# A fourth softmax tile, and slope tables made by halving the one before, in a differential-attention decoder layer

## Chip, core and metric

The kernel runs on one core of a Trainium2 chip. The metric is the device time of one execution in microseconds (us), as the median of several runs. Beside it stands one profiled execution, whose trace gives every instruction's start and duration.

## What is computed

One decoder layer over 1024 tokens of width 1024: three branches (differential attention, pooling, cross-attention to 256 memory tokens), merged by gates and an output product, then a channel mixer. All is float32. The change touches the differential attention alone (8 heads, two softmax maps per head, width 64 each):

```python
def one_block(args):                    # 128 queries at a time
    qblk, i = args
    qpos = i * Q_BLOCK + jnp.arange(Q_BLOCK)
    s = jnp.einsum('bqhcd,bkhcd->bhcqk', qblk, kf) * scale
    dist = qpos[:, None] - kpos[None, :]
    bias = -slopes[:, None, None] * dist.astype(jnp.float32)   # slopes: 2 ** -(h + 1)
    s = s + bias[None, :, None]
    s = jnp.where((dist >= 0)[None, None, None], s, jnp.finfo(jnp.float32).min)
    p = jax.nn.softmax(s, axis=-1)
    a = p[:, :, 0] - lam * p[:, :, 1]
    return jnp.einsum('bhqk,bkhe->bqhe', a, vf)
```

Each head's output is then normalized per token, and all heads enter one product (the attention branch's merge).

## The kernel before

Each matmul of the layer's large products is done as three products of rounded halves (`mm3`, lines 103 to 105, high x high, low x high, high x low). A framework places the tiles and schedules: the code names the instructions, and a list scheduler with estimated durations sets the order in which they stand on each engine's queue; each engine then runs its queue strictly in that order and waits where an operand or a buffer is not ready. `tc.issue_after` adds edges by hand.

Attention runs head by head (h = 0 to 7). A head has eight query blocks of 128 tokens, t = 2b + u, in four pairs b; block t sees n = (t + 1) x 128 keys, so the last blocks of a head have n = 896 and n = 1024. For a block:

- `products` (L1185, tile `pss`): TensorE makes both maps' scores, c = 0 and 1, each in a pair of PSUM banks. There are two such pairs (`ps2`, bufs 2).
- `scores` (L1210): VectorE adds the head's slope table `hbias` to the scores, writes the sum into the SBUF tile `z` (tag `z0` for the first map, `z1` for the second), and keeps the row minimum in `mx`. In `order` rows this instruction is ISA, in the profile CUSTOM_DVE_ANT_0. Then ScalarE takes the exponential in place (L1219) and sums the row.
- `combine` (L1236 to L1239): VectorE subtracts the second map, weighted, from the first, into the first map's tile. That tile (`z0`) therefore lives on until the block's weights are transposed; the second map's (`z1`) is free after the combine.
- `turn_weights` (L1255, tile `pta`): TensorE transposes the pair's weights in groups of up to four into PSUM banks (`ps1`, two banks, shared with `poa` and `pn`); ScalarE copies a group rounded (L99, `aT`), VectorE subtracts for the low half (L100), which frees the bank.
- `weigh_values` (L1274, `poa`): TensorE weighs the values; ScalarE copies the output and its square (L1276, L1280, L1282).
- `head_norm` (L1299, `pn`): sums of squares by a product with ones; ScalarE copies the row (L1301) and GpSimd's queue stores it.

Pair b's transposes and weighing stand a stage behind its scores, and the next head's first blocks follow without a break. Between them the scheduler spreads filler products: the next head's keys (`head_keys`, L103 to L105 into `pqk`, 24 matmuls for each half of the tokens; `hTh_110` is the first half, `hTh_111` the second), and gates (`gate`, into `pg`) in head 0, in head 7 and after it. After attention the heads' outputs are loaded, scaled (L1527) and split into `ath` and `atl`, and the merge (`pya`) begins.

The slope tables: GpSimd makes `bias` once (L1060, L1062), a table of minus-distances with a huge value where a key lies ahead of the query. For each head ScalarE makes a scaled copy, `hbias` (L1067, two buffers), one head ahead: head h + 1's in stage b = 1 of head h. All these tiles are in the pool `att`: `bias` and `hbias` 4608 bytes per partition each, a `z` 4096 bytes; there were three `z0` and two `z1`.

Of the kernel before, what the change touches and what calls it, by code (L numbers as in the profile page):

```python
# [8 lines left out]
F32 = mybir.dt.float32  # L9
F32R = mybir.dt.float32r  # L10
I32 = mybir.dt.int32
AF = mybir.ActivationFunctionType
# [3 lines left out]
P = 128  # L16
D = 1024
S = 1024
# [23 lines left out]
def kernel(  # L42
# [7 lines left out]
    nc = tc.nc  # L50
# [12 lines left out]
    out = out[0]  # L63
# [293 lines left out]
    with tc.tile_pool(name="kvm", reuse_waits="tile", bufs=1, side="right") as kvp:  # L357
# [5 lines left out]
        with tc.tile_pool(name="pa", reuse_waits="tile", bufs=2, side="right") as pa, \  # L363
# [22 lines left out]
            with tc.issue_after(begun.ins):  # L386
                table = nc.scalar.activation(out=small.tile([P, 1], F32, tag="sm", name="table"), in_=epsilon,
                                             func=AF.Sqrt)
# [82 lines left out]
            for i in range(2):  # L471
                on("dve", lambda: nc.vector.tensor_scalar(
                    out=rcol[:, i, :], in0=ident, scalar1=0.0, scalar2=rm[i], op0=ALU.mult, op1=ALU.add))
# [581 lines left out]
    ap_ = cstack.enter_context(tc.tile_pool(name="att", reuse_waits="tile", bufs=3, side="right"))  # L1055
    vpool = cstack.enter_context(tc.tile_pool(name="vp", reuse_waits="tile", bufs=2, side="right"))


    bias = ap_.tile([P, 1152], F32, name="bias", bufs=1)
    nc.gpsimd.iota(bias, pattern=[[-1, 1152]], base=896, channel_multiplier=1,  # L1060
                   allow_small_or_imprecise_dtypes=True)
    nc.gpsimd.affine_select(out=bias, in_=bias, compare_op=ALU.is_ge, fill=-NEG, base=896,  # L1062
# [1 line left out]

    def head_bias(h):
        biases[h] = ap_.tile([P, 1152], F32, tag="hbias", name="hbias", bufs=2)
        return nc.scalar.activation(out=biases[h], in_=bias, func=AF.Copy, scale=2.0 ** -(h + 1))  # L1067

    ones = ap_.tile([P, P], F32R, name="ones", bufs=1)
    nc.gpsimd.memset(ones.bitcast(F32), 1.0)  # L1070
# [94 lines left out]
    biases = {}  # L1165
# [5 lines left out]
    def products(h, b, u):  # L1171

        t = 2 * b + u
        n = (t + 1) * P
        parts = 1 if n <= H else 2
        m = n // parts
        q = qts[h, t // 4]
        ts = slice((t % 4) * P, (t % 4 + 1) * P)
        maps[h, b, u] = []
        for c in range(2):  # L1180
            pss = bank2(name="pss2")
            for i in range(parts):
                keys = kts[h][c][:, i * m:(i + 1) * m]
                for j in range(2):
                    last["scores"] = nc.tensor.matmul(pss[:, i * H:i * H + m], q[:, j, c, ts], keys,  # L1185
                                                      start=(j == 0), stop=(j == 1))
            maps[h, b, u].append(pss)
            marks["map", c] = last["scores"]
        if b == 3 and u == 1:
            kts.pop(h)  # L1190

    def scores(h, b, u, behind=None):

        if (h, b, u) not in maps:
            products(h, b, u)
        t = 2 * b + u
        n = (t + 1) * P
        parts = 1 if n <= H else 2
        m = n // parts
        mx = small.tile([P, 2], F32, tag="mx", name="mx")  # L1200
        sm = small.tile([P, 1], F32, tag="sm", name="sm")
        z2 = []

        def halves(a):
            return a.rearrange("p (a m) -> p a m", a=parts)

        for c, pss in enumerate(maps.pop((h, b, u))):
            z = ap_.tile([P, S], F32, tag="z%d" % c, name="z", bufs=3 - c)
            o = 896 - t * P
            last["min"] = nc.vector.tensor_tensor_reduce(  # L1210
                out=halves(z[:, 0:n]), in0=pss.rearrange("p (a m) -> p a m", a=2)[:, 0:parts, 0:m],
                in1=halves(biases[h][:, o:o + n]), scale=1.0, scalar=3.0e38,
                op0=ALU.add, op1=ALU.min, accum_out=mx[:, c:c + 1])
            z2.append(z)

        def exponentials(behind=behind):
            with tc.issue_after(behind.ins) if behind else nullcontext():
                for c, z in enumerate(z2):
                    last["exp"] = nc.scalar.activation(out=z[:, 0:n], in_=z[:, 0:n], func=AF.Exp, scale=-1.0,  # L1219
                                                       bias=mx[:, c:c + 1],  # L1220
                                                       accum_out=sm if c else sums[:, h, t:t + 1])
            exps[h, b, u] = z2, mx, sm
            if (h, b, u) == (NH - 1, 0, 1):
                calm.extend((last["min"], last["exp"]))

        if h and (b, u) == (0, 0):
            held.append(exponentials)
        else:
            exponentials()
# [112 lines left out]
    with tc.issue_after(head_bias(0).ins):  # L1342
        late[0]()
# [13 lines left out]
    for h in range(NH):  # L1357
        stages = []
        for b in range(4):
            n = 4 * h + b  # L1360
            if n == 0:
                def first_scores():
                    scores(0, 0, 0)
                    next(first)
                stages.append(first_scores)
            else:
                def map0(h=h, b=b):
                    with tc.issue_after(last["gate"].ins) if h == 0 else nullcontext():
                        scores(h, b, 0)
                    if h == 0 and b < 3:  # L1370
                        next(gates[4])
                stages.append(map0)
# [5 lines left out]
            if b == 1 and h + 1 < NH:  # L1378
                def slopes(h=h):
                    with tc.issue_after(last["exp"].ins):  # L1380
                        head_bias(h + 1)
                stages.append(slopes)
# [17 lines left out]
            def map1(h=h, b=b):  # L1400
                with tc.issue_after(last["gate"].ins) if h == 0 and b < 3 else nullcontext():
                    scores(h, b, 1)
                for _ in range(0 if h else 2 if b == 3 else 1):
                    next(gates[4])
# [223 lines left out]
    with tc.tile_pool(name="wo", reuse_waits="tile", bufs=1, side="right") as wo:  # L1628
# [7 lines left out]
        for t in range(KT):  # L1636
            i, c = t // 4, (t % 4) * P
# [315 lines left out]
```

## Time and profile before

| | before |
|---|---|
| median of 3 runs | 1723.15 us (1721.95 to 1723.34) |
| the profiled execution's own time | 1723.77 us |
| its span, first to last instruction | 1722.0 us |
| TensorE matmul busy in the span | 1707.8 us, 99% |
| VectorE busy | 1249.3 us, 73% |
| ScalarE busy | 892.5 us, 52% |
| granted TensorE clock, mean | 0.999 |
| attention's stretch, first minimum to the first merge product | about 620 to 903 us |

The profiled execution is 1.8 us longer than its span (what lies before the first and after the last instruction), and 0.62 us above the median of the runs. PE is TensorE's matmuls, PEld its weight loads, DVE VectorE, ACT ScalarE, POOL GpSimd, SP the engine that issues most transfers. In a row of the timeline the first two numbers are start and duration in us; a row that ends in x8 merges eight instructions. A wait row reads: who waited, for whom, us in total, times, longest. The end of a matmul is modelled, so the starts say more than the durations.

### The profile page before, as it was taken

The page shows a single profiled execution, that of the slowest core. Times are in us where ns is not written, and L with a number is a line of the kernel's source. Part 1 is how long each engine was busy: PE and PEld are TensorE (multiplying, and loading weights), DVE is VectorE, ACT ScalarE, POOL GpSimd, SP SyncE. Part 2 cuts the span into 40 slices and gives each one's busy share as a digit, 9 for nine tenths or more (in the row PEclk, how much of TensorE's full clock was granted, in tenths as well). Part 3 has the DMA queues.
Part 4 walks back from the last instruction along what each step waited for, and adds up shares of the span by engine and source line. Part 5 has one row for each costly group of instructions (what it writes and reads, how often), then busy time and mean ns, then how long its engine had stood idle before and what let it go on. Part 6 is the DMA issues. An engine that isn't in the chain of part 4 may idle for free.

```text
span 1722.0 us, 22407 instructions
## 1 busy us (share of the span) xinstructions
PE 1707.8 (99%) x8094; PEld 1418.1 (82%) x8094; DVE 1249.3 (73%) x2075; ACT 892.5 (52%) x1594; POOL 42.9 (2%) x99
## 2 busy tenths in 40 slices
PE   8999999999999999999999999999999999999998
PEld 6888888888888888888888878888888888888886
DVE  6676876666665668889866655848888888877466
ACT  5334454444543457887754444645555555543453
POOL 0000000000000011111110000000000000000000
PEclk9999999999999999999999999999999999999999
DMA  8765544444873496666537571562433432582344
GB/s 263 250 245 218 165 153 149 161 150 148 252 241 135 147 282 191 179 181 170 154 125 265 202 233 42 173 225 92 129 118 97 122 96 88 197 304 99 107 149 142
DMA packets 232885, 294.43 MB, mean 171 GB/s; under 512 B 15945, under 2 KB 161606, under 8 KB 230086
## 3 DMA queue, kind: packets, MB, share of 16 engines
q1 hardware_dynamic: 229558, 286.66, 51.8%
q0 software_dynamic: 3200, 6.33, 1.0%
q8 instruction: 64, 1.05, 0.2%
q14 instruction: 47, 0.39, 0.1%
q10 hardware_dynamic: 16, 0.00, 0.0%
HBM read 201.10 MB, written 85.56 MB: 166 GB/s over the span
## 4 chain that ended last, share of the span: by engine, by line
PE 92%; DVE 3%; DMA 3%; ACT 1%; issue 1%; SPq 0%; DVEq 0%; ACTq 0%
PE pa L104 8%; PE pa L105 8%; PE pa L103 8%; PE pb L104 5%; PE pb L103 5%; PE pb L105 5%; PE pss L1185 3%; PE poa L1274 3%; PE pd L103 2%; PE pd L104 2%; PE pd L105 2%; PE pta L1255 2%; PE pe L104 2%; PE pe L103 2%; PE pe L105 2%; PE pout L104 2%
## 5 line engine op out<-in xcount | busy, mean ns | idle before, releaser
L89 ACT ACTIVATE wpage<-s 128x512 fp32r<-128x512 f32 x140 | 87.8, 627 | 107.3 <-DVE s L188 34.9
L90 DVE TENSOR_TENSOR wpage<-s,wpage 128x512 fp32r<-128x512 f32 x140 | 95.4, 687 | 43.9 <-ACT wpage L89 43.8
L1720 DVE SCALAR_TENSOR_TENSOR cvt<-gv,cols,cvt 128x1023 f32<-128x1023 f32 x88 | 112.4, 1278 | 15.4 <-ACT cvt L1715 14.7
L1219 ACT ACTIVATE z<-z,mx 128x256 f32<-128x256 f32 (+7 forms) x128 | 98.8, 773 | 19.5 <-DVE mx L1210 19.1
L1210 DVE CUSTOM_DVE_ANT_0 z<-pss,hbias 128x256 f32<-128x256 f32 (+7 forms) x128 | 94.6, 752 | 14.8 <-PE pss L1185 11.5
L103 PE MATMUL pa<-T,wpage 128*128 128x512 f32 x264 | 102.8, 389 | 0.0
L105 PE MATMUL pa<-T,wpage 128*128 128x512 f32 x264 | 102.7, 389 | 0.0
L104 PE MATMUL pa<-T,wpage 128*128 128x512 f32 x264 | 102.7, 389 | 0.0
L89 ACT ACTIVATE page<-blk 128x1024 fp32r<-128x1024 f32 (+1 forms) x42 | 41.4, 989 | 83.9 <-PE pe L104 50.6
L1185 PE MATMUL pss<-ks,q 128*128 128x512 f32 (+5 forms) x384 | 84.0, 346 | 0.1
L90 DVE TENSOR_TENSOR page<-blk,page 128x1024 fp32r<-128x1024 f32 (+1 forms) x42 | 47.5, 1131 | 45.5 <-ACT page L89 45.5
L103 PE MATMUL pa<-hT,wpage 128*128 128x512 f32 x180 | 70.0, 389 | 0.0
L104 PE MATMUL pa<-hT,wpage 128*128 128x512 f32 x180 | 70.0, 389 | 0.0
L105 PE MATMUL pa<-hT,wpage 128*128 128x512 f32 x180 | 70.0, 389 | 0.0
L1185 PEld LDWEIGHTS pss<-ks,q 128*128 128x128 f32 x384 | 63.4, 188 | 7.7 <-DVE mx L1210 1.9
L103 PE MATMUL pd<-page 128*128 128x512 f32 x176 | 68.7, 390 | 0.0
L104 PE MATMUL pd<-page 128*128 128x512 f32 x176 | 68.5, 389 | 0.0
L105 PE MATMUL pd<-page 128*128 128x512 f32 x176 | 68.3, 389 | 0.0
L1274 PEld LDWEIGHTS poa<-aT,v 128*128 128x128 f32 x480 | 61.1, 190 | 3.7 <-ACT srow L1301 1.6
L1274 PE MATMUL poa<-aT,v 128*128 128x256 f32 (+1 forms) x480 | 63.5, 281 | 0.0
L103 PEld LDWEIGHTS pa<-T,wpage 128*128 128x128 f32 x264 | 49.6, 188 | 10.7 <-DVE gv L252 0.3
L105 PEld LDWEIGHTS pa<-T,wpage 128*128 128x128 f32 x264 | 49.5, 188 | 10.2
(437 smaller groups left out, 4950.2 us busy)
## 6 DMA issues: line engine op xcount, KB each, us to landing
q<-q_d SPq DMA_DIRECT2D x64, 256.0 KB, 4.4
wd<-in_w_down_dram SPq DMA_DIRECT2D x22, 512.0 KB, 5.7
tw_d<-wd SPq DMA_DIRECT2D x11, 1024.0 KB, 4.0
rawv<-in_w_up_dram SPq DMA_DIRECT2D x22, 512.0 KB, 5.6
rawu<-in_w_up_dram SPq DMA_DIRECT2D x22, 512.0 KB, 3.8
ff_d<-cvt SPq DMA_DIRECT2D x22, 512.0 KB, 4.3
blk<-ff_d SPq DMA_DIRECT2D x20, 512.0 KB, 7.9
br<-tw_d SPq DMA_DIRECT2D x20, 512.0 KB, 4.4
```

Source lines behind the costliest of these rows:

```text
L89: copy = nc.scalar.activation(out=hi, in_=src, func=AF.Copy)
L90: nc.vector.tensor_tensor(out=lo, in0=src, in1=hi.bitcast(F32), op=ALU.subtract)
L103: nc.tensor.matmul(o, ah, bh, start=first, stop=False, skip_group_check=onto)
L104: nc.tensor.matmul(o, ah, bl, start=False, stop=False, skip_group_check=onto)
L105: return nc.tensor.matmul(o, al, bh, start=False, stop=last, skip_group_check=onto)
L1185: last["scores"] = nc.tensor.matmul(pss[:, i * H:i * H + m], q[:, j, c, ts], keys, start=(j == 0), stop=(j == 1))
L1210: last["min"] = nc.vector.tensor_tensor_reduce(out=halves(z[:, 0:n]), in0=pss.rearrange("p (a m) -> p a m", a=2)[:, 0:parts, 0:m], in1=hal ...
L1219: last["exp"] = nc.scalar.activation(out=z[:, 0:n], in_=z[:, 0:n], func=AF.Exp, scale=-1.0, bias=mx[:, c:c + 1], accum_out=sm if c else su ...
L1255: nc.tensor.transpose(pt[:, j * P:(j + 1) * P], zs[u][:, k * P:(k + 1) * P], ident)
L1274: nc.tensor.matmul(po[:, qs], (vh, vl)[i][:, k, :], w[j][:, ws], start=(n == 0), stop=(n == len(terms) - 1))
L1720: nc.vector.scalar_tensor_tensor(out=cv[:, sh:], in0=u[:, 0:S - sh], scalar=w, in1=cv[:, sh:], op0=ALU.mult, op1=ALU.add)
```

## The change

Two things. The first map's score tile gets a fourth buffer (`bufs=4 - 2 * c`: four for c = 0, two for c = 1, as before). The table of positions is no longer kept beside the heads' tables: it takes one of their two buffers, and each head's table is half of the one of the head in front. Halving a power of two is exact, so the tables hold the same numbers. The pool's tiles take 512 bytes per partition less.

```diff
-    bias = ap_.tile([P, 1152], F32, name="bias", bufs=1)
+    bias = ap_.tile([P, 1152], F32, tag="hbias", name="bias", bufs=2)
...
     def head_bias(h):
         biases[h] = ap_.tile([P, 1152], F32, tag="hbias", name="hbias", bufs=2)
-        return nc.scalar.activation(out=biases[h], in_=bias, func=AF.Copy, scale=2.0 ** -(h + 1))
+        return nc.scalar.activation(out=biases[h], in_=biases.get(h - 1, bias), func=AF.Copy, scale=0.5)
...
         for c, pss in enumerate(maps.pop((h, b, u))):
-            z = ap_.tile([P, S], F32, tag="z%d" % c, name="z", bufs=3 - c)
+            z = ap_.tile([P, S], F32, tag="z%d" % c, name="z", bufs=4 - 2 * c)
```

The number of instructions on each engine is the same; the scheduler puts them in another order around the end of every head. Numbers behind a name tell buffers apart.

VectorE, from the last blocks of head 5 to head 6. `pss_7545` and `pss_7550` are the first and the second map's scores of head 5's last block (n = 1024), `aT_7556`, `aT_7565` and `aT_7574` the low halves of the three groups of transposed weights of its pair b = 2. Before:

```order
L1239 SCALAR_TENSOR_TENSOR z<-z,mx 128x768
L1210 ISA z,mx<-pss_7550,hbias 128x1024
L1210 ISA mx 128x1
L100 TENSOR_TENSOR aT_7556<-pta,aT_7555 128x512
L100 TENSOR_TENSOR aT_7565<-pta,aT_7564 128x512
L1210 ISA z,mx<-pss_7545,hbias 128x1024
L1210 ISA mx 128x1
L100 TENSOR_TENSOR aT_7574<-pta,aT_7573 128x384
```

The same place on VectorE now:

```order
L1239 SCALAR_TENSOR_TENSOR z<-z,mx 128x768
L1210 ISA z,mx<-pss_7545,hbias 128x1024
L1210 ISA mx 128x1
L1210 ISA z,mx<-pss_7550,hbias 128x1024
L1210 ISA mx 128x1
L100 TENSOR_TENSOR aT_7556<-pta,aT_7555 128x512
L100 TENSOR_TENSOR aT_7565<-pta,aT_7564 128x512
L1236 RECIPROCAL mx<-sm 128x1
L1237 SCALAR_TENSOR_TENSOR mx<-mx,sums,nlam 128x1
L1239 SCALAR_TENSOR_TENSOR z<-z,mx 128x896
L100 TENSOR_TENSOR aT_7574<-pta,aT_7573 128x384
```

The first map's minimum has moved from behind two subtractions to the front, and the combine of the block with 896 keys from behind the third subtraction to ahead of it. The first map's minimum stands earlier in the other seven heads too.

TensorE at the same turn, from a filler of the keys' product on. Before:

```order
L103 MATMUL pqk<-hTh_111,wh 128x512
L1255 MATMUL pta<-ident,z 128x128 x3
L104 MATMUL pqk<-hTl_113,wh 128x512
L1299 MATMUL pn<-sq_7520,ones 128x256
L1299 MATMUL pn<-sq_7521,ones 128x256
L105 MATMUL pqk<-hTh_111,wl 128x512
L103 MATMUL pqk<-hTh_111,wh 128x512
L104 MATMUL pqk<-hTl_113,wh 128x512
L1274 MATMUL poa<-aT_7555,v 128x256
L1274 MATMUL poa<-aT_7573,v 128x128
```

The same filler on TensorE now, and what follows:

```order
L103 MATMUL pqk<-hTh_111,wh 128x512
L104 MATMUL pqk<-hTl_113,wh 128x512
L105 MATMUL pqk<-hTh_111,wl 128x512
L103 MATMUL pqk<-hTh_111,wh 128x512
L104 MATMUL pqk<-hTl_113,wh 128x512
L1255 MATMUL pta<-ident,z 128x128 x3
L105 MATMUL pqk<-hTh_111,wl 128x512
L103 MATMUL pqk<-hTh_111,wh 128x512
L1299 MATMUL pn<-sq_7520,ones 128x256
L1299 MATMUL pn<-sq_7521,ones 128x256
L104 MATMUL pqk<-hTl_113,wh 128x512
L105 MATMUL pqk<-hTh_111,wl 128x512
```

Four fillers stand between it and the third group of transposes where none stood; one more filler (L103) and the weighing (`poa`) follow. After the weighing's second term come two fillers, the first score of head 6, and the term that reads `aT_7574`; five fillers that stood behind the weighing, ahead of head 6's first scores, are gone from there.

ScalarE, from head 0 to head 1. `aT_5315`, `aT_5324` and `aT_5333` are the three groups of head 0's pair b = 2; `z,sums` is the first map's exponential, `z,sm` the second's. Before:

```order
L99 ACTIVATE aT_5315<-pta 128x512
L1219 ACTIVATE z,sm<-z,mx 128x1024
L99 ACTIVATE aT_5324<-pta 128x512
L99 ACTIVATE aT_5333<-pta 128x384
L1158 ACTIVATE g_5361<-pg_5200 128x512
L1301 ACTIVATE srow<-pn 1x256
L1219 ACTIVATE z,sums<-z,mx 128x1024
L1276 ACTIVATE ao<-poa 128x256
L1280 ACTIVATE sq<-poa 128x256
```

The same place on ScalarE now:

```order
L99 ACTIVATE aT_5315<-pta 128x512
L1219 ACTIVATE z,sums<-z,mx 128x1024
L99 ACTIVATE aT_5324<-pta 128x512
L1219 ACTIVATE z,sm<-z,mx 128x1024
L99 ACTIVATE aT_5333<-pta 128x384
L1158 ACTIVATE g_5361<-pg_5200 128x512
L1301 ACTIVATE srow<-pn 1x256
L1276 ACTIVATE ao<-poa 128x256
```

The first map's exponential of the last block has moved from just ahead of the copies of the weighing's output (L1276, L1280) to five places earlier.

At the end of head 7 the gates' products are the fillers. Counted over TensorE's queue, the last product of the last weighing is matmul 4364 before and 4370 now, while the merge's first product is matmul 4442 in both: six more gate products stand ahead of the last weighing, and six fewer behind it.

## Prediction

> **What bounds the kernel now.** I read the page first, then the busy time by stretch, then the waits inside the stretch that the change touches.
>
> ```profile
> span 1722.0 us, 22407 instructions
> PE 1707.8 (99%) x8094; PEld 1418.1 (82%) x8094; DVE 1249.3 (73%) x2075; ACT 892.5 (52%) x1594; POOL 42.9 (2%) x99
> core 0: us, PE busy (x) PEld busy (x) DVE busy (x) ACT busy (x) POOL busy (x), PEclk, DMA share, GB/s
> 620.00:903.00 283.00, 282.28 (x1701) 244.40 (x1701) 237.52 (x615) 209.53 (x502) 38.15 (x71) 1.00 0.62 176
> 1100.00:1383.00 283.00, 283.00 (x1254) 234.39 (x1253) 228.82 (x299) 149.01 (x219) 0.00 (x0) 1.00 0.44 136
> ```
>
> The stretch from 620 to 903 us runs from the first score to the first product of the merge. TensorE is busy in 282.28 of 283.00 us of it, VectorE in 237.52, ScalarE in 209.53, and the clock is full. A busy TensorE here means that the filler products (next head's keys, gates) stand wherever attention itself would wait. Whether it waits unseen inside those records is the next question:
>
> ```profile
> PE pta L1255 <- ACT sq L1280: 0.3, 1, 0.3
> PE pta L1255 <- DVE z L1239: 0.2, 1, 0.2
> ...
> PEld pta L1255 <- DVE aT L100: 4.4, 17, 0.4
> PEld pta L1255 <- DVE z L1239: 2.6, 8, 0.6
> PEld pn L1299 <- ACT sq L1282: 2.2, 6, 0.4
> PEld pss L1185 <- DVE mx L1210: 1.9, 9, 0.3
> PEld poa L1274 <- ACT srow L1301: 1.6, 8, 0.2
> ...
> DVE z L1210 <- PE pss L1185: 11.5, 17, 2.3
> ```
>
> The products waited twice, 0.5 us in all. The weight loads waited 12.7 us in the five rows shown, mostly 0.2 to 0.4 us each, under a matmul that was still running. VectorE and ScalarE have spare time. So the stage is bound by TensorE's own work, and the change leaves that work as it is.
>
> The page "Perfetto Trace Analysis" of the Trainium skill (Identifying the Most-Contended Engine) says that matmul busy time is a bad measure of headroom, and that the busy share of weight loads is a better one. By that share the stage has 283.00 - 244.40 = 38.6 us of room; but the stretch from 1100, with no idle TensorE at all, has 283.00 - 234.39 = 48.6 us, so here the trace does not bear the share out as room: by the row the sum below stays at -0.4 us, by the rule alone a gain of many microseconds would be open.
>
> **The change part by part.** *The tables.* Eight ScalarE instructions make eight tables, as before; only their input and scale differ.
>
> ```profile
> L1067 ACT ACTIVATE hbias<-bias 128x1152 f32<-128x1152 f32 x8 | 9.2, 1152 | 0.0
> 610.83 1.61 POOL L1062 TENSOR_SCALAR_AFFINE_SELECT bias<-bias 128x1152 f32<-128x1152 f32 x1
> 616.00 1.15 ACT L1067 ACTIVATE hbias<-bias 128x1152 f32<-128x1152 f32 x1
> ```
>
> Same shape, 1152 ns each: 8 x 0 = 0 us. Each now reads the table that ScalarE itself wrote a head earlier, and overwrites one that was last read a head ago, as before: no new wait. The first table starts at 616.00, 3.56 us after GpSimd's select ends (612.44), so even a select that is late by 3.5 us is hidden behind ScalarE's own queue. (GpSimd's fill of the ones, ahead of the select, gets a wait for a load of the memory's key weights, which is one of the program's first.)
>
> *The fourth tile.* With three tiles, the first map's minimum of a head's last score block (128x1024) needs the tile of three blocks back, which is free only when that block's pair has been transposed. It therefore stands behind the second map's minimum and two subtractions; with four tiles it stands ahead of them (order shown above). The turn from head 5 to head 6 in the trace of before:
>
> ```profile
> 802.07 1.01 DVE L1239 SCALAR_TENSOR_TENSOR z<-z,mx 128x768 f32<-128x768 f32 x1
> 803.22 1.22 DVE L1210 CUSTOM_DVE_ANT_0 z<-pss,hbias 128x1024 f32<-128x1024 f32 x1
> 804.37 1.28 DVE L100 TENSOR_TENSOR aT<-pta,aT 128x512 fp32r<-128x512 f32 x2
> 805.57 1.21 DVE L1210 CUSTOM_DVE_ANT_0 z<-pss,hbias 128x1024 f32<-128x1024 f32 x1
> 806.71 0.55 DVE L100 TENSOR_TENSOR aT<-pta,aT 128x384 fp32r<-128x384 f32 x1
> 807.62 1.15 DVE L1239 SCALAR_TENSOR_TENSOR z<-z,mx 128x896 f32<-128x896 f32 x1
> ...
> 803.71 1.09 ACT L99 ACTIVATE aT<-pta 128x512 fp32r<-128x512 f32 x2 [0.73 <-PE pta L1255]
> 804.68 1.16 ACT L1219 ACTIVATE z<-z,mx 128x1024 f32<-128x1024 f32 x1
> ...
> 804.07 0.40 PE L105 MATMUL pqk<-hTh,wl 128*128 128x512 f32 x1
> 804.30 0.39 PE L103 MATMUL pqk<-hTh,wh 128*128 128x512 f32 x1
> 805.22 0.49 PE L1255 MATMUL pta<-ident,z 128*128 128x128 f32 x3
> 805.47 0.48 PE L104 MATMUL pqk<-hTl,wh 128*128 128x512 f32 x1
> 805.79 0.42 PE L1299 MATMUL pn<-sq,ones 128*128 128x256 f32 x2
> 806.04 0.40 PE L105 MATMUL pqk<-hTh,wl 128*128 128x512 f32 x1
> 806.75 0.37 PE L1274 MATMUL poa<-aT,v 128*128 128x256 f32 x2
> 807.47 2.06 PE L1274 MATMUL poa<-aT,v 128*128 128x128 f32 x16
> 810.93 1.06 PE L1255 MATMUL pta<-ident,z 128*128 128x128 f32 x8
> ```
>
> Now the new order with these durations. VectorE is free at 803.08 (802.07 + 1.01) and takes the first map's minimum, 1.15 us from start to next start; the second's begins at 804.23, the first subtraction at 805.38. It ends near 806.0 instead of 805.0, and with it the PSUM bank that the third group of transposes (x3) needs; in before that group started 0.25 us after the subtraction's end, so it could now start at about 806.2. TensorE gets there later too: four more filler products stand ahead, 0.23 us each (804.07 to 804.30), so 805.22 + 0.92 = 806.14. Expected wait: 0.1 us.
>
> The third term of the weighing needs that group's subtraction. ScalarE: first copy to 804.25, exponential of the first map 804.4 to 805.5, second copy to 806.1, second exponential to 807.2, third copy to 807.65. VectorE: second subtraction to 806.7, two small ones, the combine of 896 (1.07 us to the next start) to 808.2, the third subtraction to 808.7. TensorE: from 806.14 the transposes (0.25, as 805.22 to 805.47), two fillers (0.32 and 0.23), the two norm products (0.25) and three fillers (0.70) bring the weighing's start to 807.9; a second term, two fillers and a score follow, and at 808.77 the third term needs what VectorE has ready at 808.75. Expected wait: 0 to 0.1 us. The fillers that stood behind the weighing are gone, but so are they from the sum: the last eight transposes come at 808.8 + 1.9 + 0.3 = 811.0 against 810.93. For the seven turns at the ends of heads 1 to 7 that is 7 x 0.1 = +0.7 us at most from these sums, and below nothing, -0.5, if the next head's scores gain from the bank that the early minimum frees (nine loads waited 1.9 us for a minimum, mostly hidden). I take +0.2, nearer the sums.
>
> *The turn from head 0 to 1* is the one with a real wait of TensorE before:
>
> ```profile
> 649.03 0.29 PE L1255 MATMUL pta<-ident,z 128*128 128x128 f32 x1
> 649.65 0.33 PE L1255 MATMUL pta<-ident,z 128*128 128x128 f32 x1 [0.33 <-ACT sq L1280]
> 650.51 0.88 PE L1255 MATMUL pta<-ident,z 128*128 128x128 f32 x6
> ```
>
> There ScalarE made the late exponential just ahead of the copies that free the bank, and the combine came late. From start to start the first transpose and the next lie 0.62 us apart, where a train of eight has 0.11 (1.06 us for eight): 0.5 us lost, 0.3 of it as idle. The second wait idles 0.2 us. Both hang on the late minimum, so the gain lies between 0 and -0.7; I take -0.6, since the early exponential clears ScalarE's queue by a whole 1.16 us.
>
> *The end.* Ahead of the last weighing stand six more gate products than before, so 6 x 0.23 = 1.4 us less cover remains for the chain from the last head norm to the first merged head.
>
> ```profile
> 898.25 1.06 ACT L89 ACTIVATE ath<-a 128x1024 fp32r<-128x1024 f32 x1 [5.56 <-DVE a L1527]
> 899.35 1.23 DVE L90 TENSOR_TENSOR atl<-a,ath 128x1024 fp32r<-128x1024 f32 x1 [1.13 <-ACT ath L89]
> 903.00 0.39 PE L104 MATMUL pya<-atl,mpage 128*128 128x512 f32 x1
> ```
>
> The operand is ready at 900.58 and used at 903.00: 2.4 us of slack, 1.0 left. Cost 0; if that cover were gone too, each further microsecond is one of the span. ScalarE now puts a gate's copy ahead of that operand; its 5.56 us of idle hold it. *DMA:* no transfer is added, dropped or resized; two key transfers of head 4 change places, one gate store moves one place on GpSimd's queue, and tiles lie 512 bytes apart from where they lay: 0.
>
> **The sum:** 0 (tables) + 0.2 (seven turns) - 0.6 (turn from head 0) + 0 (end, DMA) = -0.4 us. Of the profiled execution's 1723.77 us that leaves 1723.4; the median of the runs is 1723.15, 0.6 lower, and so 1722.7 as a median.
>
> **The rivals.** *The pair of minima stalls the transposes (slower, 0.09).* The subtraction that frees the bank is 1.0 us later at each of eight turns, and four fillers cover only 0.92. If ScalarE or VectorE is later by x than in my chain, TensorE waits x at each turn: 8x. It decides from x = 0.43 us (3.4 us in all); fully uncovered it is 8 x 1.0 = 8 us, 1731; likelier half, 1727. For it: the margin is zero in my sums. Against: the same engines kept such margins in the rows of before (no load waited over 0.6 us). The page "TensorE: Matmul & The Clock Gate" of the Trainium skill (Architectural detail) speaks for it: only weight loads are pulled ahead, matmuls stay in order, so a filler already spent cannot step in.
>
> *The waits under the matmuls are real (faster, 0.06).* The rows on transposes and scores add to 4.4 + 2.6 + 1.9 = 8.9 us; if half of them cost TensorE time and go, -4.5 us: 1718.6. Against: 282.28 of 283.00 us busy, and 0.23 us from filler to filler. The page "Perfetto Trace Analysis" of the Trainium skill (Optimization Strategy) leans this way: gaps that repeat on the engine that should be saturated can mean too few buffers. Here the gaps repeat on VectorE (11.5 us before minima), not on the engine that bounds.
>
> *The tile is not what held the minimum (no change, 0.15 of the 0.85).* Then the bank waits stay: 1723.2. Against: the order of VectorE does change at every turn. The forecast itself has 0.70.
>
> **How the numbers follow.** About 0.2% (3.4 us) is what a measurement of this kernel can tell from no change. Forecast and no change both lie within it: 0.85. The range takes the forecast, a gain of 2.5 us from hidden waits and a loss of 0.4 us a turn (+3.2): 1720.0 to 1726.0.
>
> **What would show it.** In the changed profile VectorE's minima of 128x1024 both come ahead of the first subtraction in all eight heads; TensorE stays near 282 of 283 us; the waits on L1280 and L1239 of TensorE are gone or under 0.2 us; the three transposes start about 0.9 us later after the second score block. The prediction is wrong if loads for those transposes wait over 0.4 us at most turns, or if the first merge product waits for its operand.

## The result, and the profile after

The changed kernel takes 1726.49 us as a median of 22 runs, the kernel before 1723.03 us in as many runs beside them: a ratio of 1.0021, with a 95% interval of 1.0016 to 1.0027. That is 3.6 us slower (2.8 to 4.7), where 1722.7 us was forecast, and 0.5 us above the forecast range. (Here and below the ratio is estimated from the single runs of both kernels, so it need not be the quotient of the medians.) The profiled execution takes 1725.67 us:

```profile
span 1723.9 us, 22403 instructions
PE 1710.1 (99%) x8094; PEld 1420.0 (82%) x8094; DVE 1250.0 (73%) x2075; ACT 890.4 (52%) x1594; POOL 42.9 (2%) x99
```

The page hides the loss: TensorE is as busy as before, and the span grew by 1.9 us only. The first score starts at 617.80 us here and at 620.27 before, though every engine has the same instructions in the same order up to there: that is a difference between executions, not between kernels. So I compare stretches, each from its own first instruction: attention from the first score (`pss`) to the merge's first product (`pya`), here the busy times of after and, in the second fence, of before (columns as in the prediction):

```profile
617.80:901.95 284.15, 283.21 (x1700) 244.32 (x1699) 237.23 (x613) 206.13 (x500) 38.17 (x71) 1.00 0.61 173
```

```profile
620.27:902.78 282.51, 281.79 (x1700) 244.02 (x1699) 237.42 (x614) 209.31 (x502) 38.15 (x71) 1.00 0.62 176
```

Attention is 1.64 us longer for the same 1700 matmuls. From the merge's first product to the first output product (`pout`, at 990.49 us, before at 989.82) it is 88.54 us against 87.04: 1.50 us more. Together 3.1 us; what is left to 3.6 lies within the interval.

**At the turns.** The waits of attention's weight loads in the changed kernel:

```profile
PEld pta L1255 <- DVE aT L100: 3.2, 13, 0.3
PEld pta L1255 <- ACT sq L1280: 2.7, 9, 0.4
...
PEld pss L1185 <- DVE mx L1210: 2.1, 9, 0.3
PEld poa L1274 <- ACT srow L1301: 1.6, 8, 0.2
PEld poa L1274 <- DVE aT L100: 1.5, 7, 0.3
PEld pta L1255 <- DVE z L1239: 1.5, 5, 0.6
```

The transposes wait less for the subtraction (4.4 us before) and for the combine (2.6 before). Two rows stand out: transposes that wait for the square of the weighing's output, nine times (twice before), and the weighing itself (`poa`), seven times, for a subtraction (no such row before). The turn from head 1 to head 2 shows both, TensorE first, then VectorE and ScalarE:

```profile
674.12 0.49 PE L1255 MATMUL pta<-ident,z 128*128 128x128 f32 x3
...
675.84 0.37 PE L1274 MATMUL poa<-aT,v 128*128 128x256 f32 x2
676.05 0.50 PE L1185 MATMUL pss<-ks,q 128*128 128x128 f32 x3
676.65 2.15 PE L1274 MATMUL poa<-aT,v 128*128 128x128 f32 x16
678.64 0.23 PE L1185 MATMUL pss<-ks,q 128*128 128x128 f32 x1
678.71 0.62 PE L1255 MATMUL pta<-ident,z 128*128 128x128 f32 x4
679.08 0.47 PE L103 MATMUL pqk<-hTh,wh 128*128 128x512 f32 x1
679.56 0.66 PE L1255 MATMUL pta<-ident,z 128*128 128x128 f32 x4
...
674.98 1.15 DVE L1239 SCALAR_TENSOR_TENSOR z<-z,mx 128x896 f32<-128x896 f32 x1
676.05 0.55 DVE L100 TENSOR_TENSOR aT<-pta,aT 128x384 fp32r<-128x384 f32 x1
...
678.85 0.38 ACT L1276 ACTIVATE ao<-poa 128x256 f32<-128x256 f32 x1 [3.13 <-PE poa L1274]
679.13 0.38 ACT L1280 ACTIVATE sq<-poa 128x256 f32<-128x256 f32 x1
```

The three scores take 0.33 us, so the weighing's third term could start at 676.38; it starts at 676.65, right behind the third subtraction, which ends at 676.60 because VectorE makes the combine of 896 ahead of it. The weighing ends at 678.80. Its PSUM bank comes free when ScalarE has read it twice, at 679.51 (679.13 + 0.38), and the second four transposes, which need that bank, start at 679.56. They could have started at 679.31, one filler (0.23) after 679.08. The same place before:

```profile
678.70 2.06 PE L1274 MATMUL poa<-aT,v 128*128 128x128 f32 x16
680.60 0.40 PE L104 MATMUL pqk<-hTl,wh 128*128 128x512 f32 x1
680.83 0.40 PE L105 MATMUL pqk<-hTh,wl 128*128 128x512 f32 x1
681.06 0.56 PE L1185 MATMUL pss<-ks,q 128*128 128x128 f32 x4
681.46 1.06 PE L1255 MATMUL pta<-ident,z 128*128 128x128 f32 x8
...
681.08 0.38 ACT L1280 ACTIVATE sq<-poa 128x256 f32<-128x256 f32 x1
```

There two fillers and four scores stood behind the weighing; the bank was free at 681.46 (681.08 + 0.38), and all eight transposes ran as one train of 1.06 us. By the starts of the matmuls the changed kernel loses 0.52, 0.55 and 0.67 us at the turns out of heads 1 to 3 (both waits) and 0.17, 0.16 and 0.17 out of heads 4 to 6 (the bank alone): 2.24 us. Out of head 0 it wins 0.47. Little of this is idle time of the matmul row: in the stretch TensorE is idle for 0.72 us before and 0.94 us now, and the places above show four gaps of 0.10 to 0.14 us. A late start shows as a longer gap between starts.

**At the end.** The merge's products of the first page pair, on TensorE and ScalarE, in the changed kernel:

```profile
903.76 0.39 PE L105 MATMUL pya<-ath,mpage 128*128 128x512 f32 x1
905.33 0.50 PE L103 MATMUL pya<-ath,mpage 128*128 128x512 f32 x1 [1.18 <-ACT g L1158]
...
903.22 0.63 ACT L89 ACTIVATE mpage<-rawm 128x512 fp32r<-128x512 f32 x1 [0.97 <-DMA rawm<-in_w_attn_branch_dram]
903.75 1.04 ACT L89 ACTIVATE ath<-a 128x1024 fp32r<-128x1024 f32 x1
904.70 0.58 ACT L1158 ACTIVATE g<-pg 128x512 f32<-128x512 f32 x1
```

The merge's tenth product needs a PSUM bank that still holds the last gate. The copy that empties it (`g`, L1158) stands on ScalarE behind a page that waits for its load and behind the second head's rounded copy, and ends at 905.28. TensorE was ready at 903.99, so it loses 1.34 us. ScalarE before:

```profile
902.23 0.63 ACT L89 ACTIVATE mpage<-rawm 128x512 fp32r<-128x512 f32 x1 [0.24 <-DMA rawm<-in_w_attn_branch_dram]
902.77 1.04 ACT L89 ACTIVATE ath<-a 128x1024 fp32r<-128x1024 f32 x1
903.72 0.58 ACT L1158 ACTIVATE g<-pg 128x512 f32<-128x512 f32 x1
```

The copy ended at 904.30, and the bank was needed at 902.78 + 9 x 0.227 = 904.82: half a microsecond of slack. The six gate products (1.36 us) that no longer stand behind the last weighing were that slack and more; the page ahead of the copy, too, now waits 0.97 us for its load, and 0.24 before.

### The profile page after: what moved, and what is told of

Read it like the earlier page. It is cut to its first block, busy times and chain, and to the rows that moved or that the text cites. A ratio compares the mean times of both kernels' runs of the same rounds, so it can differ in the third digit from the quotient of the medians.

```text
span 1723.9 us, 22403 instructions
## 1 busy us (share of the span) xinstructions
PE 1710.1 (99%) x8094; PEld 1420.0 (82%) x8094; DVE 1250.0 (73%) x2075; ACT 890.4 (52%) x1594; POOL 42.9 (2%) x99
## 4 chain that ended last, share of the span: by engine, by line
PE 90%; DVE 4%; DMA 3%; ACT 1%; issue 1%; SPq 0%; DVEq 0%; ACTq 0%
PE pa L104 8%; PE pa L105 8%; PE pa L103 8%; PE pb L104 5%; PE pb L103 5%; PE pb L105 5%; PE poa L1274 3%; PE pss L1185 3%; PE pd L103 2%; PE pd L104 2%; PE pd L105 2%; PE pe L104 2%; PE pe L103 2%; PE pe L105 2%; PE pout L104 2%; PE pout L105 2%
## 5 line engine op out<-in xcount | busy, mean ns | idle before, releaser
L103 PE MATMUL pa<-T,wpage 128*128 128x512 f32 x264 | 102.8, 389 | 0.0
L103 PE MATMUL pa<-hT,wpage 128*128 128x512 f32 x180 | 70.0, 389 | 0.0
L103 PE MATMUL pd<-page 128*128 128x512 f32 x176 | 68.7, 390 | 0.0
L103 PEld LDWEIGHTS pa<-T,wpage 128*128 128x128 f32 x264 | 49.5, 188 | 10.6 <-DVE gv L252 0.3
```

The costliest lines, as they stand in the source:

```text
L103: nc.tensor.matmul(o, ah, bh, start=first, stop=False, skip_group_check=onto)
```

## The experiments

The theory that I tested: the buffer and the tables cost nothing; the order that the fourth tile allows spends filler products early, and two waits that they covered come up, at the turns and at the end. The first rival: the tables or the tiles' addresses cost by themselves. The second: only one of the two places counts. For each run I give the whole time and its two stretches, attention and merge, which together took 369.55 us before and 372.69 after. The runs that add an edge in the code have line numbers one or two higher there (L1256 for L1255).

**The tables alone** (`tables`).

```diff
-            z = ap_.tile([P, S], F32, tag="z%d" % c, name="z", bufs=4 - 2 * c)
+            z = ap_.tile([P, S], F32, tag="z%d" % c, name="z", bufs=3 - c)
```

> Only the tables are changed (each head's is half of the one before, no table of positions); the first map's tile keeps three buffers, and every engine's order is that of before. Order theory: all of the loss comes from the new order that the fourth tile brings, so this is the kernel before, 1723.0 us within 1.0, with the merge's bank wait under 0.3 us. Table theory (the halved tables, or tiles that lie 512 bytes apart from where they lay, cost time by themselves): 1724.5 to 1726.5.

Measured: 1724.33 us, 1.0007 (0.9999 to 1.0016) of before; stretches 283.15 and 87.04 us. No wait at the merge. Attention holds 0.6 us more than before, all of it one late score at 621.07 us for which the profile shows no cause and which no other kernel here has:

```profile
PE pss L1185 <- issue: 0.4, 1, 0.4
```

The time lies between the two forecasts, and the interval alone leaves up to 2.8 us open. In the trace all engines have the order of before, instruction by instruction, so this late score is a difference between executions of one order. The next run narrows the bound.

**Four tiles, old order** (`late_all`, and by parts `late_h7`, `late_h06`). One edge more, with the condition of the three runs:

```diff
-            last["min"] = nc.vector.tensor_tensor_reduce(
+            with tc.issue_after(last["turned"][1].ins) if (b, u, c) == (3, 1, 0) else nullcontext():
+                last["min"] = nc.vector.tensor_tensor_reduce(
...
+            # late_h7:  ... if (b, u, c) == (3, 1, 0) and h == 7
+            # late_h06: ... if (b, u, c) == (3, 1, 0) and h < 7
```

> The changed kernel, four tiles and halved tables, but in every head the first map's minimum of the last block is held back behind the second subtraction of the turn, where it stood with three tiles. Order theory: about 1723.0 us within 1.0; the first score to the first merge product takes 282.5 us again and the merge's bank wait is gone. Theory that the tile or the tables themselves cost (addresses, one more buffer): 1726.5.

> As late_all, but the first map's minimum is held back in head 7 alone, so six gate products stand behind the last weighing again, and the turns of heads 0 to 6 stay as changed. If the loss is split as the two traces show it (about 1.6 us at the turns, 1.2 to 2 us at the merge's bank and after it): 1724.9 us, within 0.7, with attention's stretch near 284 us and no bank wait at the merge. If the turns alone cost: 1726.2. If the end alone costs: 1723.1.

> The other half: the first map's minimum is held back in heads 0 to 6, and head 7 stays as changed, with six gate products fewer behind the last weighing. If the loss is split: 1724.8 us, within 0.7, with attention's stretch near 282.6 us and a bank wait of 1.0 to 1.4 us at the merge. If the turns alone cost: 1723.2. If the end alone costs: 1726.3.

Measured: `late_all` 1723.92 us, 0.9999 (0.9990 to 1.0007); `late_h7` 1725.37, 1.0011 (1.0002 to 1.0020); `late_h06` 1725.50, 1.0014 (1.0005 to 1.0023). Their attention stretches, one fence each, in this order:

```profile
618.77:901.25 282.48, 281.73 (x1699) 243.93 (x1698) 237.12 (x614) 208.28 (x501) 38.27 (x71) 1.00 0.62 176
```

```profile
618.85:903.11 284.26, 283.30 (x1699) 244.45 (x1698) 237.96 (x614) 207.03 (x502) 38.25 (x71) 1.00 0.62 174
```

```profile
619.87:902.28 282.41, 281.67 (x1700) 243.75 (x1698) 236.46 (x613) 207.44 (x500) 38.17 (x71) 1.00 0.62 174
```

The merge takes 87.08, 87.37 and 88.63 us, and only the last has its wait:

```profile
PE pya L103 <- ACT g L1158: 1.3, 1, 1.3
```

With four tiles and the new tables, but the minimum where it stood, the kernel is the one before to within 1.2 us (the upper end of the interval), and its attention stretch to within 0.03 us: buffer, tables and addresses do not make the loss of 3.6 us. Each half of the order carries its own half of the loss, as expected.

**The gate's copy first** (`gcopy`, `before_gcopy`, `gcopy2`). In `gcopy` the splits of the fourth page and of the second head come after the last gate's copy; `before_gcopy` is the same edit of the kernel before; `gcopy2` leaves the page alone and only exchanges copy and head on ScalarE.

```diff
+            last["gcopy"] = nc.scalar.activation(out=g, in_=pg, func=AF.Copy)
...
+        with tc.issue_after(last["gcopy"].ins) if (dt, g) == (3, 0) else nullcontext():   # not in gcopy2
             split(w[:, 0], w[:, 1], raw)
...
+            with tc.issue_after(last["gcopy"].ins) if h == 1 else nullcontext():
                 split(ath[h], atl[h], a)
```

> The changed kernel, its attention untouched; the last gate's copy, which frees the merge's fourth PSUM bank, is put ahead of the second head's rounded copy and of the fourth page's on ScalarE. If the bank behind that copy is what the merge waits for: the wait of 1.2 us is gone, first merge product to first output product takes 87.1 us instead of 88.5, and the time is 1.3 us below the changed kernel, about 1725.2, with attention's stretch still near 284.2 us. If the merge only passes its wait on to the next late operand: no change, 1726.5.

> The same move of the gate's copy in the kernel before, where the bank is freed before it is needed: 1723.2 us, no change, the merge at 87.0 us. If the move by itself brings or costs something: more than 0.7 us off.

> The changed kernel with two neighbours on ScalarE exchanged and nothing else in any engine's order: the last gate's copy (0.58 us) ahead of the second head's rounded copy (1.04 us), both pages staying where they are. The bank is then free 0.95 us earlier, so the merge's wait of 1.2 us falls to 0.3 or less, the merge's stretch from 88.5 to about 87.6 us, the time to about 1725.6. If the second head's operand then comes late instead: no change, with a wait for it near 907.4.

Measured: `gcopy` 1726.11 us, 1.0017 (1.0008 to 1.0026), stretches 284.17 and 87.69; `before_gcopy` 1724.19, 1.0005 (0.9997 to 1.0014), 282.59 and 88.15; `gcopy2` 1725.30, 1.0016 (1.0007 to 1.0025), 284.18 and 87.57. `before_gcopy` cost 1.1 us in its merge, because the page that I moved back came late:

```profile
PE pya L105 <- DVE mpage L90: 0.8, 1, 0.8
```

`gcopy` waits neither for that page nor for the bank. It fell short of its 87.1 us at another place, 22.7 us into the merge, where the low half of a later page is late (in `gcopy`):

```profile
PE pya L105 <- DVE mpage L90: 0.4, 1, 0.4
```

On VectorE that half stands behind heads whose loads came late, by up to 2.4 us. `late_h7` and `late_h17`, which leave the gate's copy where it was, start 0.3 and 0.5 us late at the same product, so the edit need not be the cause.

`gcopy2` is the clean one. TensorE and ScalarE there:

```profile
904.70 0.39 PE L105 MATMUL pya<-ath,mpage 128*128 128x512 f32 x1
905.33 0.50 PE L103 MATMUL pya<-ath,mpage 128*128 128x512 f32 x1 [0.24 <-ACT g L1158]
...
904.16 0.63 ACT L89 ACTIVATE mpage<-rawm 128x512 fp32r<-128x512 f32 x1 [0.94 <-DMA rawm<-in_w_attn_branch_dram]
904.69 0.58 ACT L1158 ACTIVATE g<-pg 128x512 f32<-128x512 f32 x1
```

One exchange of two neighbours takes the wait from 1.18 to 0.24 us and the merge's stretch from 88.54 to 87.57. The bank is what the merge waited for. The whole time (1.0016 against 1.0021) moves in that direction, but the two intervals overlap.

**Fillers put back by hand** (`fill`, and with the first form of the gate's copy `fill_gcopy`), with `ends["weighed"]` the weighing's last product:

```diff
+                with tc.issue_after(ends["weighed"].ins) if i == 1 and k >= 6 else nullcontext():
                     mm3(pq, wh[:, k, :], wl[:, k, :], hTh[i][:, k, :], hTl[i][:, k, :], k == 0, k == KT - 1)
```

> The changed kernel with its early minima, but the last six products of the next head's keys are held behind the weighing at the turns of heads 1 to 6, so that they stand between the weighing and the eight transposes that need its PSUM bank. The scheduler fills the places ahead with the next head's scores. If the waits for the bank (0.16 to 0.36 us a turn) come from the fillers spent too early: no wait of the transposes for the square of the weighing's output, attention's stretch about 282.8 us, the time about 1725.1 (the merge's bank wait stays). If the late subtraction alone makes the turns slow, whatever the fillers: 284 us and 1726.5.

> Both cures at once in the changed kernel: key products held behind the weighing, and the gate's copy ahead of the head's. If the two losses are separate: attention 282.8 us, merge 87.1 us, about 1723.8 us, the kernel before again and nothing gained from the fourth tile. Below 1722.5 would mean that the early minimum is worth something once its waits are covered.

Measured: `fill` 1727.60 us, 1.0028 (1.0018 to 1.0038), 285.94 and 87.68; `fill_gcopy` 1727.66, 1.0027 (1.0016 to 1.0037), 285.99 and 88.06. Both expectations fell. The six products now cover the bank behind the weighing, and what they covered ahead of it is bare. The turn from head 5 to 6 in `fill`:

```profile
807.05 0.33 PE L1186 MATMUL pss<-ks,q 128*128 128x128 f32 x2
807.60 0.55 PE L1256 MATMUL pta<-ident,z 128*128 128x128 f32 x3 [0.21 <-DVE aT L100]
```

The three transposes start 0.4 us late, behind the subtraction that stands behind both large minima. Attention is 1.8 us slower than in the changed kernel. My reading, which no run shows by itself, is that a head has only so many fillers, and with the subtraction late they are short in one place or in the other.

**The bank freed earlier** (`sq_ao`).

```diff
-        nc.scalar.activation(out=sq, in_=po, func=AF.Square)
+        nc.scalar.activation(out=sq, in_=ao, func=AF.Square)
```

> The changed kernel, the square of the weighing's output made from its copy in SBUF instead of from the PSUM bank, so that the bank is free one ScalarE instruction (0.28 to 0.4 us) earlier; the scheduler, which knows it, moves other work too. If the bank is what the eight transposes wait for: no wait of theirs for ScalarE over 0.1 us at heads 1 to 6, attention's stretch 282.6 to 283.2 us, about 1725.2. If the fillers that this spares are again spent elsewhere: 284 us, 1726.5, with other waits.

Measured: 1728.08 us, 1.0036 (1.0022 to 1.0050), 286.38 and 88.65 us. My expectation fell, and the alternative's mechanism held, at a higher price: the scheduler, told that the bank is free sooner, used the fillers elsewhere again, and the transposes now wait for the subtraction even in the matmul row:

```profile
PE pta L1255 <- DVE aT L100: 1.0, 4, 0.3
```

Since many places moved, this run does not price the bank by itself.

**Only one early minimum** (`second_late16`: the edge of `late_all` on the second map's minimum for heads 1 to 6, on the first map's in head 7) and **the turn of head 0 alone** (`late_h17`: on the first map's in heads 1 to 7).

```diff
+            # second_late16: ... if h > 0 and (b, u, c) == ((3, 1, 0) if h == 7 else (3, 1, 1))
+            # late_h17:      ... if h > 0 and (b, u, c) == (3, 1, 0)
```

> Four tiles, but of a turn's two large minima only the first map's is early: at heads 1 to 6 the second map's is held behind the two subtractions, head 7 has the order of before, head 0 that of the changed kernel. If the loss at the turns comes from two minima ahead of the subtraction that frees the transposes' bank: attention's stretch 282.0 to 282.6 us, no waits of 0.2 us at heads 1 to 6, 1722.8 us, as before. If any order with the first map's minimum early loses its fillers: 283.5 us or more, and above 1724.5.

> Four tiles, the first map's minimum held back in heads 1 to 7 and early in head 0 alone, the one turn that had a wait of 0.5 us before. Expected: attention's stretch 0.4 to 0.5 us shorter than with all held back (282.0 us), no bank wait at the merge, 1722.8 us: nothing that the clock of a whole run can tell from before, but visible in the trace at 648 to 651 us.

Measured: `second_late16` 1724.00 us, 1.0011 (1.0003 to 1.0020), 283.45 and 87.04; `late_h17` 1721.78, 1.0002 (0.9993 to 1.0010), 281.90 and 87.58. The first missed both of its numbers: the turns out of heads 1 and 4 to 6 are clean, but out of head 2 a single filler stands ahead of the second bank (0.46 us lost), and out of head 3 the weighing waits for a row's copy and the transposes for the combine (0.22 and 0.26 us). So two minima ahead of the subtraction are not the whole of it: with one early minimum the fillers were short too, at two turns. The second has the shortest attention of all:

```profile
619.16:901.06 281.90, 281.48 (x1700) 244.06 (x1698) 237.13 (x614) 207.72 (x501) 38.13 (x71) 1.00 0.62 176
```

That is 0.58 us less than `late_all`, 0.46 of it by the starts at the turn out of head 0: the fourth tile's gain at the one turn that had a wait of its own. The merge then takes 0.5 us more than in `late_all` (87.58 against 87.08), at the late page named above, although every engine's order there is the same in both, so the two sums differ by 0.1 us only. In the whole time nothing of it can be seen. No version here is measurably faster than the kernel before.

**All kernels side by side.** The two stretches' sum, from one profiled execution each, against the whole time, from the ratio to the runs of before (ratio less one, times 1723 us):

| kernel | attention + merge, us | against before | whole time against before |
|---|---|---|---|
| late_h17 | 369.48 | -0.1 | +0.3 |
| late_all | 369.56 | 0.0 | -0.2 |
| tables | 370.19 | +0.6 | +1.2 |
| second_late16 | 370.49 | +0.9 | +1.9 |
| before_gcopy | 370.74 | +1.2 | +0.9 |
| late_h06 | 371.04 | +1.5 | +2.4 |
| late_h7 | 371.63 | +2.1 | +1.9 |
| gcopy2 | 371.75 | +2.2 | +2.8 |
| gcopy | 371.86 | +2.3 | +2.9 |
| after | 372.69 | +3.1 | +3.6 |
| fill | 373.62 | +4.1 | +4.8 |
| fill_gcopy | 374.05 | +4.5 | +4.7 |
| sq_ao | 375.03 | +5.5 | +6.2 |

The stretch sums follow the whole times within 1.0 us throughout, and each whole time has an interval of 0.9 to 2.4 us to either side. So the loss lies in these two stretches. That the order makes it is shown by `late_all` and its halves, and the bank at the merge by `gcopy2`. At the turns, the two waits are read from the traces: no run takes away one of them alone (`fill` and `sq_ao`, which were to, moved other work), and none moves the combine alone.

## Why the prediction was wrong

- **What bounds.** Right: TensorE is busy in 283.21 of 284.15 us and the clock is 1.00. But I took "busy" and a short wait row as proof of cover; of attention's loss of 1.64 us only 0.22 is idle time, and the rest hides in starts that come later.
- **Tables, DMA: 0.** Borne out by `late_all`, within its interval.
- **Seven turns, +0.2: the first failed step.** Measured +2.1 us (1.64 + 0.47, and 2.24 by the starts). The chain itself was good. The turn now lies 1.43 us earlier (its combine of 768 starts at 800.64, before at 802.07); I had the eight transposes at 811.0, so 809.57 there, and they start at 809.58; the third subtraction ends 0.05 us ahead of the third term, as forecast:

```profile
804.70 0.49 PE L1255 MATMUL pta<-ident,z 128*128 128x128 f32 x3
...
807.31 2.15 PE L1274 MATMUL poa<-aT,v 128*128 128x128 f32 x16
809.30 0.45 PE L1185 MATMUL pss<-ks,q 128*128 128x128 f32 x3
809.58 1.28 PE L1255 MATMUL pta<-ident,z 128*128 128x128 f32 x8
...
801.57 1.22 DVE L1210 CUSTOM_DVE_ANT_0 z<-pss,hbias 128x1024 f32<-128x1024 f32 x1
802.71 1.22 DVE L1210 CUSTOM_DVE_ANT_0 z<-pss,hbias 128x1024 f32<-128x1024 f32 x1
803.85 1.42 DVE L100 TENSOR_TENSOR aT<-pta,aT 128x512 fp32r<-128x512 f32 x2
806.71 0.55 DVE L100 TENSOR_TENSOR aT<-pta,aT 128x384 fp32r<-128x384 f32 x1
```

  What failed was the sentence that the fillers behind the weighing "are gone, but so are they from the sum". I followed operands up to the start of the eight transposes and did not ask what frees their second bank: ScalarE's square, 0.7 us after the weighing's end. Here the second four's weight loads wait 0.23 us for it, and the eight take 1.28 us for 1.06. And I worked out one turn and charged it seven times: out of heads 1 to 3, three scores (0.33 us) stand where the turn out of head 5 has two fillers and a score (0.67 us), which is where the third term waits 0.3 us.
- **The turn of head 0, -0.6.** Nearly right: -0.47 by the starts, and 0.58 between `late_all` and `late_h17`. But the 0.2 us of idle for the combine was not at this turn: it stands at 633.46 us before and at 631.00 after, in head 0's middle, and stayed.
- **The end, 0: the second failed step.** Measured +1.5 us. The operand that I checked was in time (ready at 901.03, needed at 902.17). The same six products also covered the bank of the last gate, and that slack was 0.5 us. My sentence that ScalarE "now puts a gate's copy ahead of that operand" looked at one gate's copy; the next one, behind the next head, decided. The parts that moved, 2.1 - 0.5 + 1.5, add to the 3.1 us of the two stretches.
- **The rivals.** "The pair of minima stalls the transposes" had the sign and, with 1727 at its likelier half, the size, at a chance of 0.09 that was too low: my own margins of zero were the reason to give it more. That its size came out is luck, since its place was wrong: the three transposes hardly waited (their row fell from 4.4 to 3.2 us), what came after them did. The sentence beside it, from "TensorE: Matmul & The Clock Gate" of the Trainium skill (Architectural detail; the order of matmuls stands under "Step-by-step: what each phase is for"), that matmuls stay in order, agrees with the trace: the filler behind the four late transposes of 679.56, for which the profile lists no wait, starts behind them, at 679.97. "The waits under the matmuls are real" fell in its sign: rows that added to 8.9 us shrank to 6.8 (3.2 + 1.5 + 2.1 us), and attention took longer. "The tile is not what held the minimum" fell: with four tiles both minima stand ahead of the first subtraction in all eight heads.
- **The test points.** The minima stand as forecast and TensorE is busy in 282.06 of 283.00 us. The points that I named as fatal were half right: the three transposes did not wait, and the first merge product had its operand. The tenth lacked its bank.

## What to carry to other kernels

Where filler work hides waits, an order that moves a step earlier spends fillers, so go through every wait that those fillers covered: operands, and also the buffers, with the instruction that frees each (its last reader, and what that reader queues behind). Do this at every place where the order differs, since a slack of 0.05 us worked out for one turn says nothing for the six others. And compare stretches between fixed instructions, not spans: here one profile of each stretch placed thirteen kernels within 1 us. A difference of less than about 0.6 us in a stretch's length can't be read from one such profile unless single starts show its place: `tables` and before, in the same order throughout, differ by 0.6 us in attention, `late_h17` and `late_all` by 0.5 us in the merge.

## What the runs showed that I had not expected

- The first score starts anywhere from 617.80 to 620.31 us in executions whose instructions up to there are in the same order (changed kernel and `tables`). That alone is more than half of the effect studied.
- A PSUM bank outlives the last product into it by 0.71 us here (678.80 to 679.51), since two ScalarE passes read it one after the other.
- When the scheduler was told of an earlier release (`sq_ao`) or of a later filler (`fill`), it moved work at most turns and lost more than the wait was worth, 2.2 and 1.8 us in attention against the changed kernel.
